# Small copies of a mixer stage moved from GpSimd to VectorE, and two tiles declared once with their padding

## The chip, the cores and the metric

One core of a Trainium2 chip runs the whole kernel. The metric is the device time of one execution in microseconds. The engines are TensorE (PE in the rows; PEld its weight loads), VectorE (DVE), ScalarE (ACT), GpSimd (POOL) and SyncE (SP), which issues most of the DMAs; POOL issues the rest. Lxxx is a line of the kernel before.

## The reference

One layer of a decoder trunk for 512 prompt tokens and 8 sequences of 4 sample tokens, 1024 channels wide. Two token mixers read the same normalized input h. What the change touches is in the two of them:

```python
# mixer A: gated depthwise convolution of width 3
bg, cg, xin, q, ... = split_columns(h @ w['w_in'])
up = jnp.concatenate([u_prev, cg * xin], axis=1)   # u_prev: zeros for the prompt, state_conv for the samples
y = bias + sum(w[k] * up[:, k:k + t] for k in range(3))
conv_new = up[:, t:]                               # the last two columns of u are an output
y_a = (bg * y) @ w['w_out_conv']
# mixer B, sample tokens: attention over compressed blocks, selected blocks and a window
p_c = softmax(q . kc - distance)    # 63 compressed blocks; blocks are chosen from sums of four neighbours
o = gate0 * (p_c @ vc) + gate1 * (p_s @ v_sel) + gate2 * (p_w @ vw)
```

The merge of both mixers, an output projection and a feed-forward network follow.

## The kernel before, in words

All linears are computed in three matmuls of 32-bit halves: a weight slab of 128 columns is split by ScalarE (L174, high part wh) and VectorE (L175, low part wl), both with two buffers, and TensorE adds up h_hi*wh, h_lo*wh and h_hi*wl (L179 to L181) over 8 blocks of channels, in two halves of 288 and 256 tokens.

The mixer stage (L707 to L941) weaves two generators. `fill_gen` makes eight passes k of `conv_gen`, one for each 128 channels. A pass is three linears, cg, x_in and bg, each in four steps of 12 matmuls. After cg, the pass takes the tile `up` (2 zero columns, 512 prompt tokens, then 8 times 2 state columns and 4 sample tokens). POOL sets the two zero columns (L734) and copies the state columns (L735); VectorE writes the product cg * x_in into the rest (L739, L740, L742); ScalarE and VectorE make the convolution (L745 to L747); POOL copies the last columns to `ncv` (L748, L749), which TensorE transposes at the end of the stage (L935). `sample_gen` makes four passes bp, two sequences each: POOL issues 16 indirect DMAs that gather cached rows (L780) and one direct load (L791), TensorE makes scores, VectorE and ScalarE the softmax parts, and POOL adds the selection bias (`bs`, L834). Column 63 of the probabilities `px` is padding that POOL sets to zero in each pass (L810), because the sums of four neighbours read 64 columns. Each `yield n` of `sample_gen` lets n steps of the linears run in between.

The tile framework keeps each engine's instructions in an order that it chooses by priority (the order of the program) and readiness, and sets all semaphore waits. `up` and `px` have one buffer, so a pass's first instruction on them waits until all accesses of the pass before are done; the first `up` lies on memory that held the q tiles of the stage before, whose stores to DRAM (L702) must be done first, and `cg` on the q tiles too. The pool gives places in the order in which tiles are declared: the state tile, ncv, cg, up, v.

The gathers of pass bp + 1 are issued after the value matmuls of the first branch of pass bp (L874), which free their buffers:

```python
        yield from branch(...)                 # selected blocks, bs as the table
        if bp < 3:
            rows_of[bp + 1] = gather(bp + 1)   # 16 indirect DMAs on POOL
        yield from branch(...)                 # window
```

Of the kernel before, what the change touches and what calls it, by code (L numbers as in the profile page):

```python
# [9 lines left out]
F32 = mybir.dt.float32  # L10
# [87 lines left out]
def build(tc, a, o):  # L98
    nc = tc.nc
    sync, act, dve, pool, pe = nc.sync, nc.scalar, nc.vector, nc.gpsimd, nc.tensor  # L100
    top = ExitStack()

    def mkpool(stack, name, space=None, side="left"):
        if space is DRAM:
            return stack.enter_context(tc.tile_pool(name=name, bufs=1, space=DRAM))
        if space is PSUM:
            return stack.enter_context(tc.tile_pool(name=name, bufs=1, space=PSUM))
        return stack.enter_context(tc.tile_pool(name=name, bufs=1, side=side, reuse_waits="tile"))
# [9 lines left out]
    def tp_ps(nm):  # L118
        return ps.tile([128, 512], F32, tag="g", bufs=5, name=nm)
# [9 lines left out]
    def nm(s):  # L129
        uid[0] += 1  # L130
        return f"{s}_{uid[0]}"
# [25 lines left out]
    def raw_tile(n):  # L157
        return wpool.tile([128, 2048], F32, tag="raw", bufs=3, name=nm(n))
# [9 lines left out]
    def split(view, nk=8, perm=None):  # L168
        wh = wpool.tile([128, 8, 128], F32R, tag="wh", bufs=2, name=nm("wh"))
        wl = wpool.tile([128, 8, 128], F32R, tag="wl", bufs=2, name=nm("wl"))  # L170
        oh, ol = wh[:, 0:nk, :], wl[:, 0:nk, :]
        if perm is not None:
            oh, ol = perm(oh), perm(ol)
        act.activation(oh, view, AF.Copy)  # L174
        dve.tensor_sub(ol, view, oh.bitcast(F32))  # L175
        return wh[:, 0:nk, :], wl[:, 0:nk, :]
# [15 lines left out]
    def linear_gen(w, x, ev):  # L192

        wh, wl = w
        xh, xl = x
        for hf in range(2):
            p = lin_ps(nm("lin"))[:, 0:HW[hf]]
            for k in range(KC):
                mm3(p, wh, wl, xh[:, k, hcols(hf)], xl[:, k, hcols(hf)], k, k == 0, k == KC - 1)
                if k == KC - 1:  # L200
                    ev(hf, p)
                if k % 4 == 3:
                    yield

    def hcols(hf):
        return slice(*HS[hf])
# [153 lines left out]
    for j in range(4):  # L360
        t = wpool.tile([128, D], F32, tag=("wh", "wl")[j % 2], bufs=2, name=f"xr{j}")
# [136 lines left out]
    for j in range(4):  # L498
        for q in range(2):
            p = tp_ps(nm("xtp"))  # L500
# [3 lines left out]
    p = tp_ps(nm("xtp"))  # L504
# [167 lines left out]
    p = tp_ps("gtp")  # L672
# [5 lines left out]
    for gp in range(2):  # L678
        for rp_ in range(2):
            t = raw_tile("rq")  # L680
# [29 lines left out]
    cv = mkpool(cst2, "cv", side="right")  # L710
    smp = mkpool(cst2, "smp", side="right")
# [10 lines left out]
    stT = cv.tile([128, 8, 16], F32, name="stT")  # L722
    sync.dma_start(stT.rearrange("p k n -> p (k n)"), a["state_conv"])
    ncv = cv.tile([128, 8, 18], F32, name="ncv")

    conv_w = {}

    def conv_gen(k):
        cs = slice((k % 2) * 128, (k % 2) * 128 + 128)
        cg = cv.tile([128, NT], F32, tag="cg", bufs=1, name=nm("cg"))  # L730
        yield from linear_gen(split(slab_for("cg", k)[:, :, cs]), h, lambda hf, p: act.activation(cg[:, hcols(hf)], p, AF.Copy))
        up = cv.tile([128, 562], F32, tag="up", bufs=1, name=nm("up"))
        us = up[:, 514:562].rearrange("p (b t) -> p b t", t=6)
        pool.memset(up[:, 0:2], 0.0)  # L734
        pool.tensor_copy(us[:, :, 0:2], stT[:, k, :].rearrange("p (b t) -> p b t", t=2))  # L735

        def ev_x(hf, p):
            if hf == 0:
                dve.tensor_mul(us[:, :, 2:6], p[:, 0:TS].rearrange("p (b t) -> p b t", t=4), cg[:, 0:TS].rearrange("p (b t) -> p b t", t=4))  # L739
                dve.tensor_mul(up[:, 2:258], p[:, TS:288], cg[:, TS:288])  # L740
            else:
                dve.tensor_mul(up[:, 258:514], p, cg[:, 288:NT])  # L742
        yield from linear_gen(split(slab_for("xin", k)[:, :, cs]), h, ev_x)
        v = cv.tile([128, 560], F32, tag="v", bufs=1, name=nm("v"))
        act.activation(v, up[:, 0:560], AF.Identity, scale=wconvT[:, 0, k:k + 1], bias=bconvT[:, k:k + 1])  # L745
        dve.scalar_tensor_tensor(v, up[:, 1:561], wconvT[:, 1, k:k + 1], v, ALU.mult, ALU.add)
        dve.scalar_tensor_tensor(v, up[:, 2:562], wconvT[:, 2, k:k + 1], v, ALU.mult, ALU.add)  # L747
        pool.tensor_copy(ncv[:, k, 0:2], up[:, 512:514])  # L748
        pool.tensor_copy(ncv[:, k, 2:18].rearrange("p (b t) -> p b t", t=2), us[:, :, 4:6])  # L749

        def ev_b(hf, p):
            if hf == 0:
                pv = p[:, 0:TS].rearrange("p (b t) -> p b t", t=4)
                vv = v[:, 512:560].rearrange("p (b t) -> p b t", t=6)[:, :, 2:6]
                dve.tensor_mul(yinf[:, k, 0:TS].rearrange("p (b t) -> p b t", t=4), pv, vv)
                dve.tensor_mul(yinf[:, k, TS:288], p[:, TS:288], v[:, 0:256])
            else:
                dve.tensor_mul(yinf[:, k, 288:NT], p, v[:, 256:512])
        yield from linear_gen(split(slab_for("bg", k)[:, :, cs]), h, ev_b)

    def slab_for(nme, k):
        if k % 2 == 0:
            conv_w[nme] = slab(a["w_in"], {"cg": C_CG, "xin": C_XIN, "bg": C_BG}[nme] + k * 128)
        return conv_w[nme]
# [4 lines left out]
    def small(w_, n):  # L769
        return smp.tile([128, w_], F32, tag=f"sm_{n}", bufs=2, name=nm(n))  # L770
# [15 lines left out]
    def sample_gen(bp):  # L786
# [14 lines left out]
        for b2, gp, rows in quads:  # L801
            pe.matmul(xs_[rows, 64:128], lhsT=qbd[:, b0 + b2, gp, :], rhs=kn[:, gp].rearrange("p x n -> p (x n)"), start=True, stop=True)
        sx = smp.tile([128, 128], F32, tag="sx", bufs=1, name=nm("sxs"))
        px = smp.tile([128, 128], F32, tag="px", bufs=1, name=nm("px"))
        n5 = small(5, "n5")
        softmax_part(sx[:, 0:63], xs_[:, 0:63], t_cmp[:, 0:63], n5[:, 0:1])
        softmax_part(sx[:, 64:96], xs_[:, 64:96], t_new[:, bp * 32:bp * 32 + 32], n5[:, 1:2])
        softmax_part(sx[:, 96:128], xs_[:, 96:128], t_new[:, bp * 32:bp * 32 + 32], n5[:, 2:3])
        sm = small(6, "sm")
        pool.memset(px[:, 63:64], 0.0)  # L810
        act.activation(px[:, 0:63], sx[:, 0:63], AF.Exp, scale=-1.0, bias=n5[:, 0:1], accum_out=sm[:, 0:1])
        rc = small(1, "rc")
        dve.reciprocal(rc, sm[:, 0:1])
# [103 lines left out]
    def fill_gen():  # L917
        for k in range(KC):
            yield from conv_gen(k)
        for k in range(GAF):  # L920
            yield from ga_linear(k)
# [4 lines left out]
    for bp in range(4):  # L926
        for n in sample_gen(bp):
            for _ in range(n):
                next(fill, None)
    for _ in fill:  # L930
        pass
    for half in range(2):
        p = tp_ps(nm("ncp"))
# [56 lines left out]
    for k2 in range(4):  # L990
        y_a(k2)
        if k2 == 1:
            for br in range(2):
                t = at1.tile([128, 4, 256], F32, name=f"vtok{br}")
# [178 lines left out]
    for k2 in range(4):  # L1173
        t = raw_tile("wo")
# [6 lines left out]
        for kk in range(2):  # L1181
            k = k2 * 2 + kk
# [245 lines left out]
```

## Time and profile before

| what | value |
|---|---|
| median of 3 runs | 1364.76 us (1364.71 to 1367.26) |
| the profiled execution's own time | 1364.51 us |
| its span, first to last instruction | 1362.5 us |
| mean granted TensorE clock of the span | 0.978 |
| TensorE, VectorE, ScalarE, POOL busy | 96%, 47%, 38%, 9% |
| mixer stage | about 300 to 540 us |

Busy shares are averages over stages with different limits, and an engine that is off the chain may wait or work without a cost. The page's part on the chain says which engine held up the end; the waits of a stretch say who waited for whom; the timeline says in which order. Matmuls are pipelined, and their ends are modelled. A wait put down to "issue" ended on nothing that the profile shows, one put down to "remote" on an event that it cannot name.

### The profile page before, as it was taken

Reading aid. Unit: us, or ns where it says so; the run is one execution under the profiler, and the core shown is the slowest. Engines: PE = TensorE matmul, PEld = TensorE weight load, DVE = VectorE, ACT = ScalarE, POOL = GpSimd, SP = SyncE. Lnnn points to the kernel's source line nnn. Section 1 sums busy time; section 2 is a strip of 40 time slices with the busy share of each in tenths; the row PEclk is TensorE's granted clock in tenths of the full one; section 3 lists DMA queues with packets and bytes.
Section 4 is the critical chain, followed back from the end, with each engine's and each line's share of the span. In section 5 each row is a group of like instructions: output and inputs, shape, how many; then the busy total and the mean of one; then the engine's idle time right before and its main releaser. Section 6 shows DMA issues by size and latency. Waiting matters only on the chain.

```text
span 1362.5 us, 25289 instructions
## 1 busy us (share of the span) xinstructions
PE 1301.3 (96%) x10640; PEld 1200.7 (88%) x10640; DVE 636.3 (47%) x1543; ACT 521.2 (38%) x1039; POOL 121.7 (9%) x175
## 2 busy tenths in 40 slices
PE   6999999899797889799999999999999999999997
PEld 5788899799696879799777787999999999999997
DVE  5459232134342434423776675666533333323335
ACT  6335233233121223322776677444432322322223
POOL 2111032300513420000000000000000000000000
PEclk9999999899898989899999999999999999999998
DMA  9995036864645544532375445451122313222321
GB/s 329 321 353 208 9 126 207 253 211 154 188 164 175 174 136 150 141 124 77 123 198 135 135 125 156 142 164 36 59 93 75 112 63 99 80 87 86 86 63 66
DMA packets 142039, 193.54 MB, mean 142 GB/s; under 512 B 5649, under 2 KB 125721, under 8 KB 137958
## 3 DMA queue, kind: packets, MB, share of 16 engines
q1 hardware_dynamic: 133414, 149.98, 35.5%
q0 software_dynamic: 8512, 41.95, 9.0%
q8 instruction: 83, 1.36, 0.4%
q14 instruction: 30, 0.25, 0.1%
HBM read 174.47 MB, written 25.76 MB: 147 GB/s over the span
## 4 chain that ended last, share of the span: by engine, by line
PE 94%; issue 2%; DMA 1%; DVE 1%; ACT 0%; SPq 0%; DVEq 0%; ACTq 0%
PE lin L179 19%; PE lin L181 19%; PE lin L180 19%; PE dn L180 3%; PE dn L179 3%; PE dn L181 3%; PE acc L1107 3%; PE ptp L1113 3%; PE phi L457 2%; PE phi L456 2%; PE phi L455 2%; PE xt L441 2%; PE modp L227 2%; PE sp L1082 1%; PE sp L1083 1%
## 5 line engine op out<-in xcount | busy, mean ns | idle before, releaser
L179 PE MATMUL lin<-h_hi,wh 128*128 128x288 f32 (+1 forms) x1648 | 481.1, 292 | 12.0 <-issue 11.9
L180 PE MATMUL lin<-h_lo,wh 128*128 128x288 f32 (+1 forms) x1648 | 478.8, 291 | 10.7 <-issue 10.7
L181 PE MATMUL lin<-h_hi,wl 128*128 128x288 f32 (+1 forms) x1648 | 479.6, 291 | 7.0 <-issue 6.8
L179 PEld LDWEIGHTS lin<-h_hi,wh 128*128 128x128 f32 x1648 | 314.5, 191 | 19.2 <-issue 15.4
L180 PEld LDWEIGHTS lin<-h_lo,wh 128*128 128x128 f32 x1648 | 313.8, 191 | 14.4 <-issue 14.0
L181 PEld LDWEIGHTS lin<-h_hi,wl 128*128 128x128 f32 x1648 | 313.6, 190 | 10.4 <-issue 10.1
L174 ACT ACTIVATE wh<-raw 128x1024 fp32r<-128x1024 f32 x132 | 137.9, 1045 | 363.9 <-PE lin L180 238.7
L175 DVE TENSOR_TENSOR wl<-raw,wh 128x1024 fp32r<-128x1024 f32 x132 | 159.1, 1206 | 251.4 <-ACT wh L174 247.5
L179 PE MATMUL dn<-f_hi,wh 128*128 128x256 f32 (+1 forms) x352 | 101.7, 289 | 0.0
L180 PE MATMUL dn<-f_lo,wh 128*128 128x256 f32 (+1 forms) x352 | 101.4, 288 | 0.0
L181 PE MATMUL dn<-f_hi,wl 128*128 128x256 f32 (+1 forms) x352 | 101.2, 287 | 0.0
L1089 ACT ACTIVATE P<-P,nms 128x512 f32<-128x512 f32 (+3 forms) x128 | 70.6, 555 | 18.8 <-DVE nms L1088 18.1
L1088 DVE CUSTOM_DVE_ANT_0 P<-sp,ta 128x512 f32<-128x512 f32 (+3 forms) x128 | 57.6, 482 | 31.1 <-PE sp L1076 23.5
L780 POOL DMA_INDIRECT sraw<-in_cache_sel,ixs x64 | 64.0, 999 | 51.9 <-PE sacc L874 32.5
L179 PEld LDWEIGHTS dn<-f_hi,wh 128*128 128x128 f32 x352 | 66.5, 189 | 0.0
L181 PEld LDWEIGHTS dn<-f_hi,wl 128*128 128x128 f32 x352 | 66.2, 188 | 0.0
L180 PEld LDWEIGHTS dn<-f_lo,wh 128*128 128x128 f32 x352 | 66.2, 188 | 0.0
L455 PE MATMUL phi<-xh,wph 128*128 128x512 f32 x128 | 53.1, 414 | 0.2 <-ACT wph L397 0.2
L456 PE MATMUL phi<-xh,wpl 128*128 128x512 f32 x128 | 51.3, 401 | 0.2 <-DVE wpl L398 0.2
L457 PE MATMUL phi<-xl,wph 128*128 128x512 f32 x128 | 51.3, 402 | 0.0
L443 ACT ACTIVATE xh<-xt 128x512 fp32r<-128x512 f32 x64 | 35.0, 597 | 33.0 <-PE xt L441 30.6
L444 DVE TENSOR_TENSOR xl<-xt,xh 128x512 fp32r<-128x512 f32 x64 | 41.2, 685 | 13.3 <-ACT xh L443 13.3
(360 smaller groups left out, 2053.9 us busy)
## 6 DMA issues: line engine op xcount, KB each, us to landing
raw<-in_w_in SPq DMA_DIRECT2D x26, 1024.0 KB
raw<-in_w_ada SPq DMA_DIRECT2D x24, 1024.0 KB
raw<-in_w_gate SPq DMA_DIRECT2D x11, 1024.0 KB
raw<-in_w_up SPq DMA_DIRECT2D x11, 1024.0 KB
wraw<-in_cache_winT POOLq DMA_DIRECT2D x4, 2048.0 KB
raw<-in_w_down SPq DMA_DIRECT2D x8, 1024.0 KB
out_new_win_sample<-in_cache_win SPq DMA_DIRECT2D x8, 1016.0 KB
rq<-in_w_in SPq DMA_DIRECT2D x8, 512.0 KB
```

The source lines that it names most:

```text
L174: act.activation(oh, view, AF.Copy)
L175: dve.tensor_sub(ol, view, oh.bitcast(F32))
L179: pe.matmul(p, lhsT=wh[:, k, :], rhs=xh, start=start, stop=False)
L180: pe.matmul(p, lhsT=wh[:, k, :], rhs=xl, start=False, stop=False)
L181: pe.matmul(p, lhsT=wl[:, k, :], rhs=xh, start=False, stop=stop)
L444: dve.tensor_sub(xlb[v][:, lp * 512:lp * 512 + 512], p, xo.bitcast(F32))
L455: pe.matmul(po, lhsT=w_h, rhs=mh, start=first, stop=False)
L456: pe.matmul(po, lhsT=w_l, rhs=mh, start=False, stop=False)
L457: pe.matmul(po, lhsT=w_h, rhs=ml, start=False, stop=last)
L780: pool.indirect_dma_start(out=t[:, pg, :], out_offset=None, in_=a["cache_sel"], in_offset=bass.IndirectOffsetOnAxis(ap=ixs[:, col:col + 1] ...
L1088: dve.tensor_tensor_reduce(out=t[:, 0:n], in0=sps[br], in1=t_dist[:, 512 - n:512], scale=-hs, scalar=3e38, op0=ALU.add, op1=ALU.min, accum ...
L1089: act.activation(t[:, 0:n], t[:, 0:n], AF.Exp, scale=-1.0, bias=nms[:, c:c + 1], accum_out=sums[:, c:c + 1])
```

## The change

The four copies and memsets of a pass of `conv_gen` and the memset of `px` leave POOL: the copies L735, L748 and L749 become VectorE copies, and the memsets are done once by VectorE, on tiles that are declared once ahead of the loops. `up` is now declared ahead of `cg`, and `px` right after the table tile of its pool.

```diff
--- before.py
+++ after.py
@@ -722,6 +722,10 @@
     stT = cv.tile([128, 8, 16], F32, name="stT")
     sync.dma_start(stT.rearrange("p k n -> p (k n)"), a["state_conv"])
     ncv = cv.tile([128, 8, 18], F32, name="ncv")
+    up = cv.tile([128, 562], F32, name="up")
+    dve.memset(up[:, 0:2], 0.0)
+    px = smp.tile([128, 128], F32, name="px")
+    dve.memset(px[:, 63:64], 0.0)
 
     conv_w = {}
 
@@ -729,10 +733,8 @@
         cs = slice((k % 2) * 128, (k % 2) * 128 + 128)
         cg = cv.tile([128, NT], F32, tag="cg", bufs=1, name=nm("cg"))
         yield from linear_gen(split(slab_for("cg", k)[:, :, cs]), h, lambda hf, p: act.activation(cg[:, hcols(hf)], p, AF.Copy))
-        up = cv.tile([128, 562], F32, tag="up", bufs=1, name=nm("up"))
         us = up[:, 514:562].rearrange("p (b t) -> p b t", t=6)
-        pool.memset(up[:, 0:2], 0.0)
-        pool.tensor_copy(us[:, :, 0:2], stT[:, k, :].rearrange("p (b t) -> p b t", t=2))
+        dve.tensor_copy(us[:, :, 0:2], stT[:, k, :].rearrange("p (b t) -> p b t", t=2))
 
         def ev_x(hf, p):
             if hf == 0:
@@ -745,8 +747,8 @@
         act.activation(v, up[:, 0:560], AF.Identity, scale=wconvT[:, 0, k:k + 1], bias=bconvT[:, k:k + 1])
         dve.scalar_tensor_tensor(v, up[:, 1:561], wconvT[:, 1, k:k + 1], v, ALU.mult, ALU.add)
         dve.scalar_tensor_tensor(v, up[:, 2:562], wconvT[:, 2, k:k + 1], v, ALU.mult, ALU.add)
-        pool.tensor_copy(ncv[:, k, 0:2], up[:, 512:514])
-        pool.tensor_copy(ncv[:, k, 2:18].rearrange("p (b t) -> p b t", t=2), us[:, :, 4:6])
+        dve.tensor_copy(ncv[:, k, 0:2], up[:, 512:514])
+        dve.tensor_copy(ncv[:, k, 2:18].rearrange("p (b t) -> p b t", t=2), us[:, :, 4:6])
 
         def ev_b(hf, p):
             if hf == 0:
@@ -801,13 +803,11 @@
         for b2, gp, rows in quads:
             pe.matmul(xs_[rows, 64:128], lhsT=qbd[:, b0 + b2, gp, :], rhs=kn[:, gp].rearrange("p x n -> p (x n)"), start=True, stop=True)
         sx = smp.tile([128, 128], F32, tag="sx", bufs=1, name=nm("sxs"))
-        px = smp.tile([128, 128], F32, tag="px", bufs=1, name=nm("px"))
         n5 = small(5, "n5")
         softmax_part(sx[:, 0:63], xs_[:, 0:63], t_cmp[:, 0:63], n5[:, 0:1])
         softmax_part(sx[:, 64:96], xs_[:, 64:96], t_new[:, bp * 32:bp * 32 + 32], n5[:, 1:2])
         softmax_part(sx[:, 96:128], xs_[:, 96:128], t_new[:, bp * 32:bp * 32 + 32], n5[:, 2:3])
         sm = small(6, "sm")
-        pool.memset(px[:, 63:64], 0.0)
         act.activation(px[:, 0:63], sx[:, 0:63], AF.Exp, scale=-1.0, bias=n5[:, 0:1], accum_out=sm[:, 0:1])
         rc = small(1, "rc")
         dve.reciprocal(rc, sm[:, 0:1])
```

## Rows read from the trace of the kernel before

**Rows 1.** The page: busy time, and the chain, by engine.

```profile
PE 1301.3 (96%) x10640; PEld 1200.7 (88%) x10640; DVE 636.3 (47%) x1543; ACT 521.2 (38%) x1039; POOL 121.7 (9%) x175
...
PE 94%; issue 2%; DMA 1%; DVE 1%; ACT 0%; SPq 0%; DVEq 0%; ACTq 0%
```

**Rows 2.** Windows: us, busy PE, PEld, DVE, ACT, POOL, PEclk, DMA, GB/s.

```profile
350.00:375.00 25.00, 17.34 (x129) 15.34 (x128) 6.66 (x12) 2.97 (x3) 14.38 (x19) 0.80 0.60 179
400.00:425.00 25.00, 16.84 (x168) 14.75 (x167) 6.99 (x15) 4.36 (x8) 16.08 (x20) 0.88 0.73 235
475.00:500.00 25.00, 19.17 (x162) 17.28 (x162) 8.84 (x25) 4.28 (x8) 7.29 (x13) 0.80 0.48 156
```

**Rows 3.** Waits, 300 to 540 us: us in total, times, longest us.

```profile
PE lin L179 <- issue: 11.1, 11, 1.6
...
PE lin L180 <- issue: 6.6, 8, 1.8
...
DVE S L767 <- POOL bs L834: 5.9, 8, 1.2
PE lin L181 <- issue: 5.8, 7, 1.7
...
PEld imp L817 <- POOL ncv L749: 0.8, 1, 0.8
```

**Rows 4.** Timeline of POOL: start us, us, operation [idle before <- releaser].

```profile
345.99 1.05 POOL L780 DMA_INDIRECT sraw<-in_cache_sel,ixs  x1 [10.32 <-PE sacc L874]
...
359.89 1.42 POOL L780 DMA_INDIRECT sraw<-in_cache_sel,ixs  x1 [0.31 <-issue]
...
366.61 0.20 POOL L748 COPY ncv<-up 128x2 f32<-128x2 f32 x1
```

**Rows 5.** Timeline of VectorE in the same stretch.

```profile
358.81 0.42 DVE L742 TENSOR_TENSOR up<-lin,cg 128x256 f32<-128x256 f32 x1 [8.28 <-remote]
359.25 1.23 DVE L175 TENSOR_TENSOR wl<-raw,wh 128x1024 fp32r<-128x1024 f32 x1
360.40 0.80 DVE L746 SCALAR_TENSOR_TENSOR v<-up,vec,v 128x560 f32<-128x560 f32 x1
...
368.84 0.69 DVE L140 COPY pts<-pt 128x512 f32<-128x512 f32 x1 [6.81 <-remote]
```

**Rows 6.** Source lines: count, ns min/median/max, first and last start us.

```profile
L735 POOL COPY up<-stT x8: 197/210/229, 324.6 to 505.9; 128x16 f32<-128x16 f32 x8
...
L748 POOL COPY ncv<-up x8: 185/186/202, 328.8 to 526.6; 128x2 f32<-128x2 f32 x8
...
L749 POOL COPY ncv<-up x8: 190/198/203, 328.9 to 523.6; 128x16 f32<-128x16 f32 x8
...
L780 POOL DMA_INDIRECT sraw<-in_cache_sel,ixs x64: 945/949/1647, 230.1 to 481.2; - x64
```

**Rows 7.** Two lines with small VectorE copies, same columns.

```profile
L850 DVE COPY nx<-n x8: 143/150/155, 326.4 to 509.3; 128x1 f32<-128x1 f32 x8
...
L605 DVE COPY kn<-kvT x4: 174/181/183, 193.9 to 233.1; 128x32 f32<-128x32 f32 x4
```

**Rows 8.** Timeline of TensorE: the first new linear after the gathers.

```profile
372.34 0.38 PE L179 MATMUL lin<-h_hi,wh 128*128 128x288 f32 x1
```

**Rows 9.** Timeline of POOL, ScalarE and VectorE in the first pass.

```profile
321.75 0.10 POOL L734 MEMSET up<- 128x2 f32 x1 [49.82 <-DMA q_dr1l<-ql]
324.60 0.20 POOL L735 COPY up<-stT 128x16 f32<-128x16 f32 x1 [2.75 <-DMA stT<-in_state_conv]
...
319.26 0.41 ACT L731 ACTIVATE cg<-lin 128x288 f32<-128x288 f32 x1 [2.31 <-DMA q_dr1h<-qh]
321.54 1.06 ACT L174 ACTIVATE wh<-raw 128x1024 fp32r<-128x1024 f32 x1 [1.86 <-PE lin L180]
...
322.63 1.23 DVE L175 TENSOR_TENSOR wl<-raw,wh 128x1024 fp32r<-128x1024 f32 x1 [4.26 <-ACT wh L174]
...
328.22 0.43 DVE L742 TENSOR_TENSOR up<-lin,cg 128x256 f32<-128x256 f32 x1 [1.27 <-PE lin L181]
```

## The prediction

> **What bounds the kernel now.** I read the page first: TensorE's matmuls take 1301.3 us of a span of 1362.5 us, and the chain that ended last is 94% TensorE and 1% VectorE; POOL is not on it [rows 1]. So a moved copy is worth only what TensorE waits for it. The change lies in the mixer stage, about 300 to 540 us, so that stage was read alone. Of its windows of 25 us three are thin, with 17.34, 16.84 and 19.17 us busy and mean granted clocks of 0.80, 0.88 and 0.80 between the two levels of 1.2 and 2.4 GHz [rows 2]; in each of them POOL issues gathers, and TensorE idles for 5.8 to 8.2 us. The waits of the stage then say what TensorE waited for: 11.1 + 6.6 + 5.8 = 23.5 us before matmuls of the linears, all put down to "issue", which names no engine [rows 3]. The same view has two waits that end on POOL: one weight load that waited 0.8 us for L749, and VectorE's S line, 5.9 us in 8 times, for the bs add L834 [rows 3]. Nobody else in it waits for a moved operation.
>
> The three thin windows are those of the gathers. In the first, POOL issues 16 gathers from 345.99 us, and L748 stands behind them and runs at 366.61 us [rows 4], with L749, L734 and L735 right after it. VectorE meanwhile got L742 only at 358.81 us after 8.28 us idle, and its next copy from PSUM at 368.84 us, 2.2 us after POOL is done with the gathers [rows 5]. This is a stall of all engines while gathers are issued; its cause is not named by the profile, and the change leaves the gathers, their place and what they wait for (L874) alone.
>
> **The change part by part.** *POOL loses* 8 x (100 + 210 + 186 + 198 ns) = 5.55 us of L734, L735, L748 and L749 [rows 6, 9], and 4 memsets of px (L810), at the 0.1 us of L734 0.4 us: 36 instructions, 6.0 us. On the path that is worth 0: POOL is not on the chain, and the only weight load that waited for one of them waited 0.8 us while the matmuls before it were still running. Gathers wait for TensorE, not for these copies, so they start no earlier. The bound from below is a gain of 0.8 us.
>
> *VectorE gains* 24 copies (L735, L748, L749, 8 times each) and 2 memsets. The trace has no such copy on VectorE. The nearest rows are a copy of one column, 150 ns, and a copy of 32 columns, 181 ns [rows 7]; 2 and 16 columns lie between, so I take 0.17 us for each of the 26: 4.4 us, with ends of 3.9 and 4.7 us. What VectorE must deliver to TensorE in this stage is the low half of the split weights (L175). In the gather window one ends at 359.25 + 1.23 = 360.48 us [rows 5] and TensorE comes to the next new linear at 372.34 us [rows 8], so the three copies added behind L742 and L747 have 11.9 us of cover there; outside the gathers a split is done one linear ahead. The term is 0; if this cover were gone it would be all 4.4 us.
>
> *The chain to bs.* L734 and L735 stand on POOL right before the bs add in four of the eight passes: 0.31 us each at most [rows 6, 9], 1.2 us less on the chain mk, bs, S. TensorE reaches the transposes of S only after six steps of the linears, and it has no wait put down to S in [rows 3]. So 0 again; the bound is a gain of 1.2 us, a part of VectorE's 5.9 us.
>
> *Waits that go.* With the copies on VectorE, its own L739, L742, L746 and L747 follow them in order, and ScalarE's L745 waits for one engine instead of two. No stall in the trace goes with that. What is late next after L742 is still TensorE's half of the linear.
>
> *A new wait, once.* One tile for u, declared ahead of cg, takes the place in memory that cg has now, and cg moves behind it; both then stand on the last q tiles that are being stored. Today the POOL memset of u waits for the store of ql until 321.75 us, L735 for the state until 324.60 us, while the cg evacuation ran at 319.26 us after waiting for a qh store [rows 9]. Moved to the place of u, the evacuation would start at about 321.75, 2.5 us later. Queued behind it on ScalarE is the split L174 of 321.54 us, which would slip to about 321.75 + 0.41 = 322.16 us, by 0.6 us, and with it the VectorE split of 322.63 us to about 323.3 us, done at 324.5 us. TensorE then works on the x_in linear of that pass, whose second half VectorE reads at 328.22 us [rows 9], before it needs it. The VectorE memset of u cannot hold up the writer of ql, which comes before the store; if L735 were queued ahead of that split it would hold it until 324.80, done at 326.0, still before 328. The memset of px waits for the last stores of the K/V stage, which are issued before the q linears; I take 0. SP's queue keeps its transfers, and POOL's gathers and the direct load L791 keep their order.
>
> *The gather windows.* L748, L749 and the next L735 belong behind the gathers today in the passes with odd k; on VectorE they run in the middle of them. There are three such windows, so 9 operations. A row on what a VectorE operation costs a gather: the median gather takes 0.95 us, and the one at 359.89 us, beside L746, took 1.42 us [rows 4 to 6], 0.47 us more. The lower end is that operations of 2 and 16 columns cost nothing, the upper that each costs 0.47 us: 9 x 0.47 = 4.2 us, if TensorE stalls as long as the gathers last. I take 0, because they are 5 times shorter than L746 and the usual gather shows no lengthening.
>
> The Trainium skill speaks against the change here: by SBUF — State Buffer, section Who interferes with whom, an fp32 copy of VectorE between SBUF tiles can take the port pair that it shares with GpSimd, and whoever comes second is blocked for the whole instruction. By that, the 9 copies would block descriptor writing for 9 x 0.17 = 1.5 us and the time would be 1366.0 us. The lengthened gather agrees in kind, but no row isolates it.
>
> **Sum.** 0 for the POOL side, 0 for VectorE, 0 for the first pass, 0 for the gathers. The profiled execution took 1364.51 us, span 1362.5 and 2.0 around it, and the median of the runs is 1364.76, 0.25 more. Predicted: 1364.5 us. With all gains counted (0.8 + 1.2) it is 1362.5, with all VectorE time on the path 1368.9. What a measurement of this kernel can tell from no change is 0.2%, 2.7 us.
>
> **Rivals.** *Slower, the gathers are stretched.* Place: the three gather windows. Mechanism: copies that today wait behind the gathers run among them and delay descriptor writing, while TensorE stalls until the gathers end. Price 4.2 us by the lengthened gather, so 1368.7 us; it counts as slower from 0.3 us for each of the 9 operations (2.7/9). For it: the gather of 1.42 us, and that VectorE's late copy at 368.84 us comes only behind the gathers. Against it: most gathers took 0.95 us, whatever the other engines did. Much the same time, 1368.9 us, would come if all 4.4 us of VectorE's work fell on TensorE's path. Together 0.16.
>
> *Faster, the gather windows lose less.* The three windows run the same code and lose 25 - 17.34 = 7.7, 8.2 and 5.8 us [rows 2], so where the engines stand when the stall begins moves what it costs by some 2 us each. With copies and their semaphores gone from POOL, both bad windows could come out like the good one: 1.8 + 2.3 = 4.2 us off (unrounded 1.83 + 2.33), 1360.3 us. For it: the spread. Against it: nothing in the trace shows TensorE waiting for POOL's copies there. 0.18.
>
> *The moved copies are hidden where they are, and remain hidden.* This is the forecast, 1364.5 us, 0.66. That the change doesn't do what it says is excluded by reading: the convolution writes u from column 2 on and the softmax parts write px at 0 to 62 and 64 to 127, so what is set once stays set.
>
> **How the numbers follow.** The three cases above, with 0.18, 0.66 and 0.16, are also faster, same and slower by 0.2%. The range takes in both rivals' prices: 1360.2 to 1368.9 us; what lies outside is either rival at more than its price.
>
> **What would show it.** If right: no moved line left on POOL, 24 copies of about 0.17 us on VectorE, the cg evacuation of the first pass at about 321.8 us, "issue" waits of TensorE in the stage still at 20 to 27 us, and gathers still starting with the release by L874. The slower rival would show gathers of over 1.2 us among new VectorE copies and the stall ending later; the faster one, thinner "issue" waits at the same gathers. A wait of a matmul on L175 or on ScalarE's L174 in the stage, or a VectorE memset that stands for microseconds on a store, would prove the cover argument wrong. So would a different order of TensorE's instructions, which I take as unchanged.

## The result, and the profile after

The changed kernel took 1373.1 us (median of 8 runs, 1369.87 to 1375.5), the kernel before 1365.22 us beside it (8 runs, 1364.65 to 1367.26): a ratio of 1.0056, with an interval of 1.0045 to 1.0067. So it is slower by 7.6 us (6.1 to 9.1), far more than the 0.2% that can be told from no change, and above the range of the prediction. The profiled execution took 1373.56 us, with a span of 1370.0 us, 7.5 more than before. The last four experiments, e5 to e8, ran at a time when the kernel before took longer, too (1368.8 us, 18 runs, 1365.67 to 1370.84), so they and their expected times are compared by ratio.

The page of the changed kernel, busy time and chain, answers to [rows 1].

```profile
PE 1308.5 (96%) x10640; PEld 1204.4 (88%) x10640; DVE 638.9 (47%) x1569; ACT 521.0 (38%) x1039; POOL 116.3 (8%) x139
...
PE 94%; issue 2%; DVE 2%; DMA 1%; ACT 0%; SPq 0%; DVEq 0%; ACTq 0%
```

POOL lost 36 instructions and VectorE gained 26, as said. But TensorE, with the same 10640 matmuls, is busy 7.2 us longer, and VectorE's share of the chain went from 1 to 2%. The loss is in one stretch. To find it, the start of the same instruction is compared in both traces, down the mixer stage. Of the kernel before, the timeline of TensorE in the first sample pass (L848 are the scores, L867 the transposes of S, L874 the value matmuls, L817 the block sums; each matmul of L800, L848, L874 and L817 leaves two records):

```profile
321.55 0.32 PE L800 MATMUL sx<-kcs,qbd 128*32 128x63 f32 x8
...
328.12 1.94 PE L848 MATMUL ss<-sraw,qbd 128*32 128x512 f32 x16
329.98 0.43 PE L817 MATMUL imp<-px,tb 128*128 128x64 f32 x2
...
339.95 1.03 PE L867 MATMUL pt<-ident,S 128*128 128x128 f32 x8
...
343.76 1.95 PE L874 MATMUL sacc<-sraw,pts 128*32 128x128 f32 x64
...
385.69 0.33 PE L817 MATMUL imp<-px,tb 128*128 128x64 f32 x2
```

The same view of the changed kernel (the lines of TensorE's matmuls there keep their numbers, but L800 is L802):

```profile
321.02 0.32 PE L802 MATMUL sx<-kcs,qbd 128*32 128x63 f32 x8
...
327.59 1.04 PE L848 MATMUL ss<-sraw,qbd 128*32 128x512 f32 x2
328.56 0.43 PE L817 MATMUL imp<-px,tb 128*128 128x64 f32 x2
...
329.24 1.90 PE L848 MATMUL ss<-sraw,qbd 128*32 128x512 f32 x6
...
333.66 1.05 PE L848 MATMUL ss<-sraw,qbd 128*32 128x512 f32 x4
...
337.86 1.05 PE L848 MATMUL ss<-sraw,qbd 128*32 128x512 f32 x4
...
342.82 1.07 PE L848 MATMUL ss<-wraw,qbd 128*32 128x512 f32 x8
343.70 0.29 PE L802 MATMUL sx<-kcs,qbd 128*32 128x63 f32 x8
...
346.41 1.09 PE L867 MATMUL pt<-ident,S 128*128 128x128 f32 x8 [2.31 <-DVE S L860]
...
351.80 1.96 PE L874 MATMUL sacc<-sraw,pts 128*32 128x128 f32 x64
...
392.63 0.33 PE L817 MATMUL imp<-px,tb 128*128 128x64 f32 x2
```

TensorE's instructions stand in another order, which nobody wrote: the framework chose it. From the instruction lists of the two kernels, in matmul instructions, from the first pass's sx on:

```
before   sx 8, lin 48, ss 8, imp 2, lin 72, pt 8, lin 24, sacc 32, ss(window) 4, lin 72, ...
changed  sx 8, lin 48, ss 1, imp 2, ss 3, lin 18, ss 2, lin 25, ss 2, lin 29,
         ss(window) 4, sx(next pass) 8, pt 8, lin 24, sacc 32, lin 72, ...
```

Elsewhere the order is the same, apart from that next sx, which is gone from its old place. Before, 72 linear matmuls lay between the last score and the transposes of S; now 29 do, with the window scores and the next sx.

The ledger, from the starts in the two fences. TensorE comes to sx 0.53 us earlier. From sx to pt it takes 25.39 us instead of 18.40, 7.0 more. From pt to sacc it is 5.39 instead of 3.81, 1.6 more. From sacc to the next imp it is 40.83 instead of 41.93, 1.1 less, while 1.3 us of window scores and sx (342.82 to about 344.1) have been done already. This last stretch holds the first gathers; with that work in its old place it took 41.8 to 43.7 us in the kernel before and in e2 to e7, so the 1.1 us are within its spread. Together 6.9 us at imp, and most of it stays: the third series of gathers in the stage starts 6.3 us later (468.01 against 461.71 us), and the transposes L935 at the end of the stage at 559.27 instead of 552.41 us. The other 0.6 us of the two spans lies behind them and was not followed.

What the 7.0 us are made of: the scores took 1.94 us together and now take 1.04 + 1.90 + 1.05 + 1.05 = 5.04 us, 3.1 more; the moved window scores and sx are 1.3; the wait for S is 2.3; 0.3 is left over. The waits of the changed kernel, 300 to 540 us, answer to [rows 3]; columns as there:

```profile
PE lin L179 <- issue: 7.7, 9, 1.6
PE lin L180 <- issue: 6.7, 8, 1.8
...
PE sacc L874 <- issue: 5.2, 3, 3.7
...
DVE S L769 <- POOL bs L834: 4.4, 6, 1.2
PE lin L181 <- issue: 3.5, 4, 1.1
...
PE pt L867 <- DVE S L860: 2.3, 1, 2.3
...
PEld imp L817 <- DVE ncv L750: 0.8, 1, 0.8
```

The linears' waits for "issue" are 17.9 us in sum, and 23.1 with the new ones of sacc, so what the prediction had at 20 to 27 us is still there. The new row that matters is pt for S. VectorE's own timeline says why S is late:

```profile
339.73 0.42 DVE L760 TENSOR_TENSOR yinf<-lin,v 128x256 f32<-128x256 f32 x1 [3.46 <-PE lin L181]
340.77 1.23 DVE L175 TENSOR_TENSOR wl<-raw,wh 128x1024 fp32r<-128x1024 f32 x1 [0.61 <-ACT wh L174]
341.91 0.68 DVE L769 CUSTOM_DVE_ANT_0 S<-ss,bs 128x512 f32<-128x512 f32 x1
...
345.60 0.75 DVE L860 TENSOR_SCALAR S<-S,f 128x1024 f32<-128x1024 f32 x1
```

The last scores end at 338.91 us. The softmax (L769, before L767) starts 3.0 us later, since VectorE, which the framework reordered as well, now has a product and a weight split in front of it, which wait for the linear matmuls in between; from there S takes 4.4 us, to 346.35. In the kernel before, the last step of S was this one:

```profile
338.80 0.76 DVE L860 TENSOR_SCALAR S<-S,f 128x1024 f32<-128x1024 f32 x1
```

It ended at 339.56 us, 0.4 us ahead of the transposes at 339.95. So pt did not wait for S before, but S was ready only just in time.

The 1.6 us between pt and sacc are the clock's. Windows of the changed kernel (columns as in [rows 2]):

```profile
345.00:348.00 3.00, 1.59 (x13) 1.59 (x14) 2.28 (x7) 0.46 (x1) 0.00 (x0) 0.94 0.54 185
348.00:351.00 3.00, 3.00 (x16) 3.00 (x16) 1.78 (x15) 1.26 (x5) 0.00 (x0) 0.50 0.00 0
```

In the three microseconds with the wait TensorE is busy 1.59, and in the next three it works all the time with a granted clock of 0.50, the lower of its two levels. Its linear matmuls there start 0.21 us apart from 347.7 to 350.9 us, and 0.12 us apart before and behind, so the 24 ahead of sacc take longer. The gathers start 6 to 8 us later and no longer line up with the 25 us windows of [rows 2], so these are not set side by side.

### The profile page after: what moved, and what is told of

The parts are those of the page before. It is cut to its first block, busy times and chain, and to the rows that moved or that the text cites. A ratio compares the mean times of both kernels' runs of the same rounds, so it can differ in the third digit from the quotient of the medians.

```text
span 1370.0 us, 25257 instructions
## 1 busy us (share of the span) xinstructions
PE 1308.5 (96%) x10640; PEld 1204.4 (88%) x10640; DVE 638.9 (47%) x1569; ACT 521.0 (38%) x1039; POOL 116.3 (8%) x139
## 4 chain that ended last, share of the span: by engine, by line
PE 94%; issue 2%; DVE 2%; DMA 1%; ACT 0%; SPq 0%; DVEq 0%; ACTq 0%
PE lin L179 19%; PE lin L180 19%; PE lin L181 19%; PE dn L180 3%; PE dn L181 3%; PE dn L179 3%; PE acc L1107 3%; PE ptp L1113 3%; PE phi L457 2%; PE phi L456 2%; PE phi L455 2%; PE xt L441 2%; PE modp L227 2%; PE sp L1082 1%; PE sacc L874 1%
## 5 line engine op out<-in xcount | busy, mean ns | idle before, releaser
L174 ACT ACTIVATE wh<-raw 128x1024 fp32r<-128x1024 f32 x132 | 137.9, 1045 | 375.2 <-PE lin L180 232.8
```

## The experiments

Three theories stood after this comparison. **A**: TensorE's new order is the whole loss. **B**: the copies on VectorE cost it, by stretching gathers or by delaying weight splits, and the order is beside the point. **C**: the new places of `up` and `cg` in memory hold up the first pass.

**e1: the kernel before, with nothing but the engine of one memset changed.**

```diff
-        pool.memset(px[:, 63:64], 0.0)
+        dve.memset(px[:, 63:64], 0.0)
```

> The kernel before with one edit: the memset of px column 63 in each pass goes from POOL to VectorE; the px tile stays one per pass, and all other copies stay on POOL. Theory A (the scheduler orders TensorE's instructions of the first sample pass anew once that memset no longer stands behind the gathers on POOL; order costs the time): TensorE's order is that of the kernel after, the score matmuls L848 of the first pass in four or five pieces, and the time is 1373 us (ratio 1.0045 to 1.0067). Rival B (the copies added to VectorE, or gathers stretched by them, cost the time): none of those copies is moved, so 1365 us (ratio 0.999 to 1.001). Rival C (the new places of u and cg in memory cost it): 1365 us too.

1373.49 us beside 1364.94 of before: 1.0061 (1.0048 to 1.0075), 8.3 us. One column of zeros on another engine gives the whole loss. Its timeline of TensorE:

```profile
327.78 1.04 PE L848 MATMUL ss<-sraw,qbd 128*32 128x512 f32 x2
...
348.23 1.97 PE L867 MATMUL pt<-ident,S 128*128 128x128 f32 x8 [3.93 <-DVE S L860]
```

The scores are cut (2, 6, 4, 4 records), pt waits 3.9 us for S. No copy was moved and `up` stands where it was, so neither B nor C can explain this loss. TensorE's order is that of the changed kernel, yet pt waits 3.9 us and not 2.3: the framework reordered ScalarE and VectorE, too, and here they have a convolution (L745 at 343.47 us, L746 at 344.35 us) ahead of the minimum of S (L852 at 345.07 us). So A has to be read as the new order of the first pass, led by TensorE's; no run changed the order of the other two engines alone.

**e2: everything else of the change, px untouched.**

```diff
+    up = cv.tile([128, 562], F32, name="up")
+    dve.memset(up[:, 0:2], 0.0)
...
-        pool.tensor_copy(us[:, :, 0:2], ...)
+        dve.tensor_copy(us[:, :, 0:2], ...)
...
-        pool.tensor_copy(ncv[:, k, 0:2], ...)
+        dve.tensor_copy(ncv[:, k, 0:2], ...)
...
```

> The change without its px part: u is one tile declared ahead of cg with its memset once on VectorE, and the copies of L735, L748 and L749 run on VectorE; px keeps one tile and one POOL memset per pass. Theory A (order of TensorE's instructions): order as in the kernel before, so 1365 us, ratio 0.998 to 1.002. Rival B (VectorE's added copies and stretched gathers): all of them are there, so 1369 to 1373 us, ratio 1.003 or more. Rival C (places of u and cg): they are as in the kernel after, so 1373 us.

1366.4 us, 1.0006 (0.9997 to 1.0015): no difference that can be told, with pt at 340.25 us and no wait for S. B and C fall as causes of the loss: the copies and the places cost at most 2.0 us by this interval, and that may be nothing.

**e3: the changed kernel, with px as one tile set once, but on GpSimd and at the old place, behind the gathers.**

```diff
-    dve.memset(px[:, 63:64], 0.0)
...
+        if bp == 0:
+            pool.memset(px[:, 63:64], 0.0)
```

> The kernel after with one instruction put back: px is still one tile with its padding set once, but the memset runs on POOL in the first pass, at its old place behind the gathers. Theory A: TensorE's order is that of the kernel before, so 1365 us, ratio 0.998 to 1.002, although 36 of the moved or dropped instructions stay away from POOL. Rivals B and C: 1372 to 1373 us, since everything that they blame is unchanged.

1365.17 us, 1.0003 (0.9994 to 1.0012). The whole change, but for the place of one memset, costs nothing that can be told (at most 1.6 us). TensorE's timeline is the old one:

```profile
328.21 1.94 PE L849 MATMUL ss<-sraw,qbd 128*32 128x512 f32 x16
...
340.05 1.03 PE L868 MATMUL pt<-ident,S 128*128 128x128 f32 x8
```

**e4: the changed kernel as it is, with its order put back by two edges.**

```diff
+                    with tc.issue_after(sacc_last[0].ins) if bp == 0 and br == 2 else ExitStack():
+                        ss_last[0] = pe.matmul(p[rows, :], lhsT=qbd[...], rhs=keys(b2, gp, q4), ...)
...
+                if ss_last[0] is not None and not held[0]:
+                    held[0] = True
+                    with tc.issue_after(ss_last[0].ins):
+                        next(fill, None)
```

The first keeps the window scores of the first pass behind its sacc, the second keeps the next linear step behind the eight scores.

> The kernel after, every operation on the engine where the change puts it, with two ordering edges that make no wait: the linear steps that follow the first pass's score matmuls are issued behind them, and the score matmuls of its window branch behind its value matmuls. TensorE's sequence of matmuls is then that of the kernel before. Theory A: 1365 us, ratio 0.998 to 1.002; no wait of the transposes for S in the first pass, gathers from about 345.5 us. Rivals B and C: 1372 to 1373 us. If it lies between, say 1369, the order is part of the cost only.

1366.52 us, 1.0015 (1.0006 to 1.0024), 2.0 us: of the loss of 8.3 us in e1, beside the same runs of before, three quarters are gone, with the memset still on VectorE. Two things are not as before. The imp matmuls stand behind the first score, not the eighth, which cuts the scores once. And VectorE has a product that waits for the linears (L760, 337.67 us) ahead of the softmax's minimum, and ScalarE a weight split (L174, 337.62 us) ahead of the Exp of S (338.58 us), so S is later and pt waits a little:

```profile
329.48 1.93 PE L851 MATMUL ss<-sraw,qbd 128*32 128x512 f32 x14
...
341.54 1.09 PE L870 MATMUL pt<-ident,S 128*128 128x128 f32 x8 [0.71 <-DVE S L863]
```

That is 0.98 us for the first score alone (327.83 to the imp matmul at 328.81) and 0.71 us for S, in sum about 1.7 of the 2.0 us.

So A holds, as it is read under e1. The next four kernels ask what in the order costs the time: that the selected branch's scores come cut and late (A1), or that window scores and sx run ahead of pt (A2); how much is the cut and how much the lateness; and whether the memset's engine or its place decides (D).

**e5: the changed kernel with the first of the two edges alone.** In e4's diff, the second part is left out. Order: ss 1, imp 2, ss 3, lin 18, ss 2, lin 25, ss 2, lin 29, pt.

> The changed kernel with one edge: the window branch's score matmuls of the first pass wait for its last sacc again, so TensorE keeps the scores in pieces between linear matmuls (1, 3, 2, 2 of the 8) and only the window scores and the next pass's sx go back to their old places. Theory A1 (the loss is the scores of the selected branch, cut in pieces and late, so S is late): the loss stays, 1372 to 1375 us; the wait of pt (L870) for VectorE's S grows from 2.3 to about 3.5 to 4 us, because the 1.0 us of window scores and the 0.5 us of sx no longer lie under it, and that work comes later instead. Rival A2 (the loss is the window scores and the next sx running ahead of S's transposes): the time returns to 1365 to 1367 us.

1.0062 (1.0046 to 1.0077), 8.5 us: the loss stays, as A1 said. The wait, and the window behind it, in this run:

```profile
PE pt L870 <- DVE S L863: 3.5, 1, 3.5
```

```profile
348.00:351.00 3.00, 3.00 (x17) 3.00 (x16) 0.40 (x1) 0.60 (x1) 0.00 (x0) 0.56 0.02 5
```

The wait grew by 1.2 us when the 1.3 us of window scores and sx no longer lay under it. So work running ahead was no part of the loss, but a cover for it. A2 falls.

**e6: the second edge alone.** Order: ss 1, imp 2, ss 7, lin 72, ss(window) 1, pt.

> The changed kernel with the other edge: the first linear matmul after the scores of the first pass is issued behind the last of the 8 scores, so the scores stand together again ahead of the 72 linear matmuls; one of the four window scores may still run early (ahead of pt). A1: 1365.5 to 1367.5 us, the 16 score records back at 1.9 to 2.9 us and pt's wait for S under 1 us. A2: most of the loss would go too, as only one window score is early, but the next sx also stands in its old place here, so the run against e5_window_only decides: by A2 e5_window_only is fast, by A1 only this one is.

1.0007 (0.9997 to 1.0016), 1.0 us, which can't be told from none; 14 score records take 1.93 us, and pt does not wait for S (the one window score ahead of it, 0.98 us, lies where e4 waited 0.71). The time was 1370.21 us, above the 1367.5 expected, beside 1368.8 of before; only the ratio answers to it. Keeping the scores together and early takes away all of the loss that can be told, though the first score is still cut off.

**e7: the scores together, but late.** The window edge stays, and the eight scores stand behind 48 of the 72 linear matmuls.

```diff
+            if bp == 0 and br == 1:
+                yield 4
+            edge = {1: lin_last, 2: sacc_last}[br] if bp == 0 else None
...
+                    with tc.issue_after(edge[0].ins) if edge else ExitStack():
+                        pe.matmul(p[rows, :], lhsT=qbd[...], rhs=keys(b2, gp, q4), ...)
...
-            yield wait
+            yield wait - 4 if bp == 0 and br == 1 else wait
```

> The changed kernel with the 8 scores of the first pass kept together but put behind 48 of the 72 linear matmuls, window scores and sx in their old places: late, not cut. It splits the loss of about 8 us into pieces and lateness. The scores together should take 1.9 us again (in pieces 4.8). From the last score to S in the changed kernel: 7.4 us, of which 3.0 lie behind a yinf product and the weight split on VectorE and 4.4 are the softmax itself; the 24 linear matmuls left cover about 3.1 us, so pt waits 1.3 us (softmax at once) to 4.3 us (behind the same two). If the cut costs its 2.8 us on the path: 1366.5 to 1371 us. If lateness alone makes the whole loss: 1372 to 1374 us.

1.0035 (1.0023 to 1.0047), 4.8 us (3.1 to 6.4). Its timeline of TensorE:

```profile
328.60 0.43 PE L821 MATMUL imp<-px,tb 128*128 128x64 f32 x2 [0.68 <-DVE px L818]
...
335.48 1.92 PE L856 MATMUL ss<-sraw,qbd 128*32 128x512 f32 x16
...
344.16 1.09 PE L875 MATMUL pt<-ident,S 128*128 128x128 f32 x8 [3.37 <-DVE S L868]
...
349.55 1.95 PE L882 MATMUL sacc<-sraw,pts 128*32 128x128 f32 x64
```

Uncut, the scores are back at 1.92 us. The wait is 3.4 us, within 1.3 to 4.3, and from pt to sacc it is 5.39 us again, 1.6 more than before: 3.4 + 1.6 = 5.0 us for lateness. With the scores gone from in front of it, imp also waits 0.7 us for px, a cost of this edit that e5 does not have: 5.7 us in sum by the rows, beside 4.8 (3.1 to 6.4) measured. Against e5, with nearly the same wait (3.5 us), the difference is 8.5 - 4.8 = 3.7 us, and the rows of the cut are worth 3.1. So the cut is a bit over a third of e5's loss and the lateness the rest; the intervals of the two runs leave some 2 to 3 us either way on that split. The linear matmuls hid little of S: ScalarE's Exp of S (341.20 us) stood behind the evacuation of the next linear's first half (L737, 340.89 us), which waits for just those matmuls, while the minimum that it needs was there by 339.25 us.

**e8: px as one tile, its memset still on GpSimd, but ahead of the first gathers; nothing moved to VectorE.**

```diff
+    px = smp.tile([128, 128], F32, name="px")
+    pool.memset(px[:, 63:64], 0.0)
...
-        px = smp.tile([128, 128], F32, tag="px", bufs=1, name=nm("px"))
...
-        pool.memset(px[:, 63:64], 0.0)
```

> The kernel before with px as one tile whose memset stays on GpSimd but stands ahead of the first gathers; no operation goes to VectorE. TensorE's order in the first pass is then the changed kernel's (scores 1, 3, 2, 2 among linear matmuls, window scores and next sx ahead of pt). Theory A (the order, set off by the memset's leaving its place behind the gathers in GpSimd's queue, is the whole loss): 1370 to 1374 us, pt waits 1 to 4 us for S. Rival D (the memset has to leave for VectorE to cost something, an effect of the engine): 1365 us.

1.0055 (1.0038 to 1.0072), 7.5 us; 1375.51 us beside 1368.8 of before. TensorE has the changed kernel's order (the first line is of POOL):

```profile
261.67 0.10 POOL L727 MEMSET px<- 128x1 f32 x1 [31.99 <-DMA v_dr<-stage]
...
329.92 1.05 PE L849 MATMUL ss<-sraw,qbd 128*32 128x512 f32 x2
...
350.38 1.97 PE L868 MATMUL pt<-ident,S 128*128 128x128 f32 x8 [3.93 <-DVE S L861]
```

For the order it is not the engine that counts: the old order came in every kernel with the memset behind the first gathers in GpSimd's queue (before, e2, e3), the new one in every kernel without an added edge where it stands elsewhere (changed, e1, e8). D falls. The 7.5 us are less clean: ahead of the gathers the memset waits 32.0 us for a store (the first line) and holds them back, to 262.42 us instead of 230.06, so late gathers are in this time, too. They were all issued by 283.1 us and no score waited for them, but TensorE came to sx at 323.36 us, 1.8 later than before.

What stays open is why this place turns the framework's order. No trace shows what the framework reckoned. One reading fits, but it is argued only. The pieces follow the gathered data: in the instruction list of the changed kernel the first four scores (1 + 3) read the first sequence's tile and the last four (2 + 2) the second's, as if those rows were expected one after the other. On the chip the gathers had all been issued by 250.7 us, some 77 us before the first score, and no score matmul waited for them. In the kernel before, the memset itself ran at 271.84 us, 50 us before sx, after a wait of 19.9 us for a store and not for the gathers. A memset behind the gathers in GpSimd's queue would hold the pass back, in such a reckoning, until the gathers are through, and the scores would then be ready together; without it the pass is laid out earlier than the rows are expected. No kernel was run that changes only what the framework expects of a gather.

No version here beats the kernel before: e2 and e3 are equal to it within what can be told, e3 with 35 instructions less on GpSimd (its expected text says 36).

## Why the prediction was wrong, point by point

- **The step that failed** is the one that the prediction's last sentence takes as given, "a different order of TensorE's instructions, which I take as unchanged". With it went the step on the chain to bs, "TensorE reaches the transposes of S only after six steps of the linears, and it has no wait put down to S": six steps are 72 matmuls; in the changed kernel 29 are left, and pt waits 2.3 us for S. That no wait was put down to S was read as cover; how much cover there was, 0.4 us, was not.
- **The term that was mis-sized** is the px memset (L810). It was counted as 4 x 0.1 us of POOL's time and worth 0; moving it alone cost 8.3 us in e1. Its own time never mattered. It was weighed only as work and as a holder of waits; its third role, as a place in a queue by which the order of the other engines is chosen, was left out, although the order is chosen by readiness.
- **The copies, and the places of the tiles, cost 0.** Right within what can be told: e2 and e3, both within 0.2% of before. The gain of 0.8 us that was the bound did not come, as the weight load L817 now waits as long for VectorE's L750. The median copy takes the 0.17 us that was read off neighbouring rows; source lines of the changed kernel, to be set beside [rows 6]:

```profile
L737 DVE COPY up<-stT x8: 165/168/341, 325.9 to 512.6; 128x16 f32<-128x16 f32 x8
...
L750 DVE COPY ncv<-up x8: 156/164/314, 328.2 to 533.5; 128x2 f32<-128x2 f32 x8
...
L782 POOL DMA_INDIRECT sraw<-in_cache_sel,ixs x64: 942/946/1640, 229.7 to 487.1; - x64
```

- **The slower rival** had the sign but not the mechanism. The median gather is 946 ns, before 949, and the timeline of the changed kernel shows a long gather, and a moved copy inside another one:

```profile
362.86 1.45 POOL L782 DMA_INDIRECT sraw<-in_cache_sel,ixs  x1 [0.30 <-issue]
363.41 0.80 DVE L748 SCALAR_TENSOR_TENSOR v<-up,vec,v 128x560 f32<-128x560 f32 x1
...
414.23 0.95 POOL L782 DMA_INDIRECT sraw<-in_cache_sel,ixs  x1 [0.30 <-issue]
...
414.84 0.34 DVE L751 COPY ncv<-up 128x16 f32<-128x16 f32 x1
```

Six moved copies ran inside a gather (not nine), and all six gathers kept their 0.94 to 0.95 us; it was the copy that took longer in four of them, 0.31 to 0.34 us. The long gather stands again beside the convolution's first 0.80 us operation (L748, before L746), as in [rows 4, 5]. The price of 0.47 us was read off that row rightly, but it belongs to the long operation and not to a copy. By the Trainium skill, SBUF — State Buffer, section Who interferes with whom, the copies could have blocked GpSimd, which the prediction put at an estimated 1.5 us. The trace shows no gather held up by a copy; where the two met, the copy, which came second, took longer. e2's interval, up to 2.0 us, would be too wide to tell this by the time alone.

- **The faster rival**: POOL free of copies did not make the gather windows lose less by an amount that shows. From sacc to the next imp, with the first gathers in between, 1.1 us were saved, within the spread of that stretch and with 1.3 us of work moved out of it, and in e3, with POOL as free and the old order, that stretch takes 41.81 us (343.85 to 385.66) instead of 41.93. The price itself was misread: the three windows of 25 us do not hold the same work, as the third series of gathers begins at 461.71 us, ahead of the window 475 to 500. Over 30 us from 1 us before the first gather of each series, TensorE is busy 22.34, 20.81 and 21.97 us, so it loses 7.7, 9.2 and 8.0 us, and there is no window that loses 5.8.
- **The chain to bs** gave nothing, as said, but not because its gain was hidden: it was not eased at all. VectorE's S line waits 4.4 us for POOL's bs in 6 times instead of 5.9 in 8; the two that are gone are those of the first pass (1.22 and 0.30 us before), whose scores now come later than bs. In e2 and e3, with the copies moved and the old order, the wait is 5.9 us in 8 times again.
- **The new wait of the first pass** came as said, and smaller. The rows of the changed kernel that answer to [rows 9]:

```profile
321.15 0.06 DVE L726 MEMSET up<- 128x2 f32 x1 [3.31 <-DMA q_dr1l<-ql]
...
321.19 0.41 ACT L735 ACTIVATE cg<-lin 128x288 f32<-128x288 f32 x1 [4.76 <-PE lin L181]
321.50 1.05 ACT L174 ACTIVATE wh<-raw 128x1024 fp32r<-128x1024 f32 x1
...
322.58 1.23 DVE L175 TENSOR_TENSOR wl<-raw,wh 128x1024 fp32r<-128x1024 f32 x1 [1.34 <-ACT wh L174]
```

The cg evacuation slipped from 319.26 to 321.19 us (321.75 was said), and the splits behind it did not slip, at 321.50 and 322.58 us instead of the 322.16 and 323.3 us said; TensorE's sx even started 0.5 us earlier. The VectorE memset in the first line stood 3.3 us on the store of ql, one of the signs that the prediction had named against its cover argument; it cost nothing that can be told, for the same memset waits 3.4 us in e3.

## What to carry to other kernels

Where a framework chooses the order of the instructions by readiness, even an operation of 0.06 us can hold a place by which other engines are ordered: before an edit is costed at nothing, the order of the bounding engine's instructions is compared in both versions. Here the place was one in a queue that holds slow DMA issues. A change that loses time for no visible reason is split by the order first (one edge that puts it back), and then by its edits one at a time; here that left one memset, and for the copies nothing that could be told. The cure is an edge between the instructions whose order matters, or leaving that one operation where it was.

## What the runs showed of the hardware

Score matmuls that write 32 rows each do not cost by their number. From start to the start of what follows, one alone took 0.97 us (327.59 to 328.56), two 0.98 (333.66 to 334.64), the four window scores before 0.97 (345.53 to 346.50), the three behind the first 1.83 (329.24 to 331.07), and all eight together 1.86 us before (328.12 to 329.98). One or two cost as much as four, which write four different groups of 32 rows; of the three, two write the same 32 rows by the instruction list, and they cost as much as eight. So a cut costs although no work is added. The Trainium skill, TensorEngine Tiling (Array Packing), section Key Properties, says that tiles work independently and can run in parallel. The 16 records together agree, and the pieces show the other side of it: a score alone takes as long as four side by side.

A wait of a few microseconds cost more than itself. In the three kernels in which pt waited 2.3 to 3.5 us (the changed one, e5, e7), the same 8 transposes and 24 linear matmuls behind it took 5.4 us to sacc instead of 3.8 (e7: 344.16 to 349.55), at a granted clock of 0.50 to 0.56 in the windows that cover most of them. With a wait of 0.7 us (e4) or none, the stretch took 3.8 to 3.9 us; with 3.9 us (e1, e8), 6.5 and 6.2 us.
